# Rows of the split weights at four distances from the activations' edge

## The chip, the core and the metric

One Trainium2 chip, of which the kernel uses one core. A core has a matrix engine (TensorE, PE in the profile; its weight loads are listed apart as PEld), a vector engine (DVE), a scalar engine (ACT), a general engine (POOL) and a queue that starts transfers (SP). All of them read and write SBUF, the memory on the core, which has 128 partitions; PE writes its results to PSUM. The metric is the device time of one execution in microseconds (us); lower is better.

## The reference

Two blocks of a model are computed in float32 for 256 tokens of width 2048. The first block is attention with a window and a SwiGLU, the second a gated recurrence (mLSTM, computed here in one piece for the 256 tokens) and an attention over a band of chunks. Cut to its large products:

```
qkv = rms_norm(x, mixer_norm) @ w_qkv;   x = x + attention(qkv) @ w_o
h = rms_norm(x, ffn_norm)
x = x + (silu(h @ w_gate) * (h @ w_up)) @ w_down
proj = modulate(rmsnorm(x, g_pre[0])) @ a_w_in        # 2048 x 16400
x = x + gate0 * rmsnorm(mlstm(proj) @ a_w_out, g_post[0])
kv = modulate(rmsnorm(x, kv_g)) @ kv_w;   qz = modulate(rmsnorm(x, g_pre[1])) @ b_w_in
x = x + gate1 * rmsnorm(band_attention(qz, kv) @ b_w_out, g_post[1])
```

The shifts, scales and gates are products of one row (silu(c)) with 2048 x 6144 and 2048 x 4096 matrices, and are made on DVE, not on PE.

## The kernel before

**Split products.** Each float32 weight matrix is cut into pieces of 256 rows by 512 columns (a slot). A slot is loaded into a tile `w` of 128 partitions x 2 x 512 (4096 bytes in a partition). ACT writes its rounded half `wh` (type fp32r), DVE the rest `wl = w - wh`. The activations lie in four tiles of 128 x 16 x 256, split in the same way: `xh`, `xl` (a normalised input, transposed) and `ah`, `al` (the output of a mixer or of the SwiGLU). A product is then three matmuls: high by high, high by low, low by high.

**Two modes** (`products`, L267 to L281). In mode tok a row of `wh` or `wl` (512 columns, 2048 bytes in a partition) is streamed past 128 columns of the activations, which are the loaded weights of the matmul; the profile writes this `mm<-wh,xh` (streamed operand first, loaded one second), 128x512. A slot gives 12 such matmuls: 2 rows, 2 halves of the tokens, 3 products. In mode wst a row of the activations (256 columns, 1024 bytes) is streamed past 128 columns of `wh` or `wl`; the profile writes `mm<-xh,wh`, 128x256. A slot gives 24 such matmuls. Each matmul has one weight load of 128 x 128.

**Buffers.** `w` has 3 buffers, `wh` and `wl` 4 each (L151, L153), used in turn: slot j of the stream uses buffer j mod 4. The tiles `xh`, `xl`, `ah`, `al`, `big` (16384 bytes each in a partition), `w`, `wh`, `wl` and `mvt` (4096 bytes each) follow each other in SBUF, so every row of `wh` and `wl` begins a multiple of 512 bytes behind the first byte of `xh` (the activations' edge). The tiles behind them are smaller. Three kinds that take part in fp32r matmuls do not stand on such a multiple, in the program as built: `acch` and `accl` begin 192 bytes past a multiple of 256 behind that edge, `onesr` 128 bytes, and the `wgh`, `wgl` of `gates_task` 160 bytes.

**What sets the order.** The stream of slots is a list fixed in the program (`order`, `plan`); between two matmuls of the stream, `pump` puts in work of background tasks (attention, transposes, gates), by a simple clock kept while the program is written. Two such tasks return below. `mv_reduce` (L378) sums a partial result over partitions with two fp32r matmuls, `bg<-acch,onesr` and `bg<-accl,onesr`. `gates_task` does 48 fp32r matmuls of 256 columns with only 40 columns of loaded weights, `bg<-xh,wgh`.

**The end.** The last product (`b_w_out`, mode tok) is finished by `fin_half` (L1235): ACT squares a piece of the result and sums it (`sumsq`, L458; the squares themselves go to a tile `sq` that nobody reads), DVE multiplies by the gate.

All engine instructions stand on line 66 in the profile, the line of the helper that issues them; they are told apart by their tiles.

```
            wh = strm.tile([P, SL, CW], F32R, tag="wh", bufs=4, name="wh")
            S.copy(wh, w)
            wl = strm.tile([P, SL, CW], F32R, tag="wl", bufs=4, name="wl")
            V.tensor_sub(wl, w, wh.bitcast(F32))
```

Of the kernel before, what the change touches and what calls it, by code (L numbers as in the profile page):

```python
# [10 lines left out]
F32 = mybir.dt.float32  # L11
F32R = mybir.dt.float32r
# [6 lines left out]
P = 128  # L19
# [2 lines left out]
KD = D // P  # L22
SL = 2
CW = 512
NEG = -1.0e30
EPS = 1e-6
DFF = 5632
# [53 lines left out]
def kernel(ctx: ExitStack, tc: tile.TileContext, i: dict, out: bass.AP):  # L81
# [6 lines left out]
    strm = ctx.enter_context(tc.tile_pool(name="strm", bufs=1))  # L88
    rest = ctx.enter_context(tc.tile_pool(name="rest", bufs=1))
    small = ctx.enter_context(tc.tile_pool(name="small", bufs=4))  # L90
    psp = ctx.enter_context(tc.tile_pool(name="psp", bufs=8, space=PSUM))

    live = [0, 0]
    mmres = [4]
    ver = {"x": [0] * KD, "a": [0] * KD}
# [21 lines left out]
    xh = keep.tile([P, KD, T], F32R, name="xh")  # L117
# [20 lines left out]
    def stream_load(upto):  # L138
        while cnt["load"] < min(upto, len(order)):
            ch, s = order[cnt["load"]]  # L140
            w = strm.tile([P, SL, CW], F32, tag="w", bufs=3, name="w")
            ch.load(s, w)
# [3 lines left out]
    def stream_split(upto):  # L146
        while cnt["split"] < min(upto, len(order)):
            j = cnt["split"]
            w = loaded.pop(j)
            clk.cur = 0.0  # L150
            wh = strm.tile([P, SL, CW], F32R, tag="wh", bufs=4, name="wh")  # L151
            S.copy(wh, w)
            wl = strm.tile([P, SL, CW], F32R, tag="wl", bufs=4, name="wl")  # L153
            V.tensor_sub(wl, w, wh.bitcast(F32))
            split[j] = (wh, wl, clk.cur)
            cnt["split"] += 1
# [54 lines left out]
    def wload(w, r0, c0):  # L211
        def f(s, t):
            a = w[r0 + s * SL * P:r0 + (s + 1) * SL * P, c0:c0 + CW]
            nc.sync.dma_start(out=t, in_=a.rearrange("(k p) n -> p k n", p=P))
# [11 lines left out]
    def do_group(idxs):  # L226
        staged = len(idxs) > 1
        ch, s0 = order[idxs[0]]
        for k in range(s0 * SL, (s0 + len(idxs)) * SL):
            while ver[ch.need[0]][k] < ch.need[1][k]:  # L230
                stall()
        stream_load(idxs[0] + 1 + PF)
        stream_split(idxs[0] + 1 + SP)
        if s0 == 0:
            shp = [P, CW] if ch.mode == "tok" else [P, 2, T]
            while live[0] + live[1] > 6:
# [3 lines left out]
        for ts in ((0,), (1,)) if staged else ((0, 1),):  # L240
            for j, idx in enumerate(idxs):
                s = order[idx][1]
                if j and ts[0]:
                    stream_load(idx + 1 + PF)
                    stream_split(idx + SP)
                wh, wl, t_w = split.pop(idx) if ts[-1] else split[idx]
                for k in range(SL):
                    kt = s * SL + k
                    clk.cur = max(t_w, rdy[ch.need[0]][kt])
                    products(ch, kt, k, wh, wl, ts)  # L250
                    ch.k = kt + ts[-1]
                    if not staged:
                        mv_step()
                    if kt < ch.nk - 1:
                        pump()
            if s == ch.ns - 1:
                clk.cur = clk.eng["pe"]
                if ch.part is not None:
                    for t in ts:
                        ch.part(ch.ps, t)  # L260
                if ts[-1]:
                    if not (ch.done and ch.done(ch.ps)):
                        mm_free()
                    ch.ps = None
                pump()
# [52 lines left out]
    def mv_jobs():  # L318
        for lab, w, c0, b, kind, dst in (
                [("A", i["ada0"], j * CW, i["ada_b"][0:1, j * CW:(j + 1) * CW], "col", (0, j // 4, j % 4))  # L320
                 for j in range(8)]
# [134 lines left out]
        return b.rearrange("p a b -> p (a b)")  # L456

    def sumsq(junk_pool, src, dst, scale=1.0):  # L458
        j = junk_pool.tile([P, CW], F32, tag="sq", bufs=1, name="sq")
        S.activation(j, src, ACTF.Square, scale=scale, accum_out=dst)  # L460

    def xt_pair(m):
# [83 lines left out]
    ssx = rest.tile([P, 2, 4], F32, name="ssx")  # L546
# [208 lines left out]
    def resid(n, ps, pool, after):  # L755
        for t in range(2):
            c = x[:, t, n * CW:(n + 1) * CW]
            V.tensor_add(c, ps[t], c)
            sumsq(pool, c, ssx[:, t, n:n + 1])
        add_bg(after(n))  # L760
# [36 lines left out]
    pools = {}  # L797
# [50 lines left out]
    def down_part(ps, t):  # L848
        c = x[:, t, 3 * CW:]
        V.tensor_add(c, ps[t], c)  # L850
        sumsq(pools["q2"], c, ssx[:, t, 3:4])
        if t:
            add_bg(xt_raw(3, raw))
# [146 lines left out]
    def num_task(h, v):  # L1000
# [22 lines left out]
        for t in range(2):  # L1023
            sumsq(q3, nm[t], ss[:, t:t + 1], scale=rd[:, t:t + 1])
# [143 lines left out]
    def band_head(g, j):  # L1168
# [5 lines left out]
        nc.sync.dma_start(out=bi, in_=bass.AP(tensor=rel.tensor, offset=h * 383, ap=[[1, P], [1, T]]))  # L1174
        G.memset(bi[0:64, 0:64], NEG)
        yield 1
# [57 lines left out]

    def fin_half(ps, t, n):  # L1235
        c = pools["yy"][:, t, n * CW:(n + 1) * CW]
        sumsq(pools["q4"], ps[t], ssx[:, t, n:n + 1])
        V.tensor_mul(c, ps[t], gt[1][:, n * CW:(n + 1) * CW])

    def fin_done(n):  # L1240
        def f(ps):
            for t in range(2):
                fin_half(ps, t, n)
        return f

    def fin_part(ps, t):
        fin_half(ps, t, 3)
        x_rstd((t,))
        for n in range(4):
            c = x[:, t, n * CW:(n + 1) * CW]  # L1250
            y = pools["yy"][:, t, n * CW:(n + 1) * CW]
            if n == 3:
                S.activation(y, y, ACTF.Copy, scale=rst[:, t:t + 1])
                G.tensor_add(c, c, y)
            else:
                V.scalar_tensor_tensor(c, y, rst[:, t:t + 1], c, op0=ALU.mult, op1=ALU.add)
        for n in range(4):
            nc.sync.dma_start(out=out[t * P:(t + 1) * P, n * CW:(n + 1) * CW], in_=x[:, t, n * CW:(n + 1) * CW])
# [39 lines left out]
    S.activation(warm, ones[:, 0:1], ACTF.Exp)  # L1298
    stream_load(1)
    stream_split(1)  # L1300
    load_x(0)
    nc.sync.dma_start(out=cols, in_=i["cols"])
# [35 lines left out]
def _lay(inputs):  # L1338
# [10 lines left out]
    r = np.arange(P)  # L1349
    lo = np.where(r[None, :] <= r[:, None], f(0), f(NEG)).astype(f)  # L1350
    up = np.where(r[None, :] > r[:, None], f(0), f(NEG)).astype(f)
    ge = np.where(r[None, :] >= r[:, None], f(0), f(NEG)).astype(f)
    inv = np.power(10000.0, -np.arange(0, 64, 2) / 64.0).astype(f)
# [33 lines left out]
```

## Time and profile before

| | |
|---|---|
| time, median of 2 runs | 2506.33 us (2505.83 to 2506.83) |
| profiled execution, its own time | 2509.79 us |
| span of the profile | 2508.0 us |
| mean granted TensorE clock | 0.989 |
| PE busy, share of the span | 97% |
| DVE busy | 70% |
| ACT busy | 48% |
| transfers | 575.63 MB, 230 GB/s |

PE's matmuls overlap each other in the profile: the duration of a matmul (389 ns, say) is not what it costs in a dense stretch. That is the distance from its start to the start of the next one. The timeline prints starts to 0.01 us, so distances below are taken over several matmuls.

### The profile page before, as it was taken

What the parts mean: (1) busy time and instruction counts of PE and PEld (TensorE: products, weight loads), DVE (VectorE), ACT (ScalarE), POOL (GpSimd) and SP (SyncE); (2) the same over time, 40 slices, a digit from 0 to 9 for tenths busy, and PEclk for the clock granted to TensorE, in tenths of its full rate; (3) what the DMA queues carried; (4) which work ended last, traced back from release to release, by engine and by line L of the source; (5) the groups of instructions that cost most, each with busy time, mean ns of one, the idle gap of its engine ahead of it and who ended that gap; (6) DMA issues with size and microseconds to landing.
All of it is one profiled execution on the core that took longest, in us unless ns stands there. A gap on an engine that the chain in (4) does not pass through costs nothing.

```text
span 2508.0 us, 34570 instructions
## 1 busy us (share of the span) xinstructions
PE 2438.4 (97%) x12782; PEld 2076.4 (83%) x12782; DVE 1752.8 (70%) x2577; ACT 1210.1 (48%) x1654; POOL 173.4 (7%) x174
## 2 busy tenths in 40 slices
PE   8989999999999999899999999999999899999998
PEld 6867888887888888778888788888888789899986
DVE  6885777777777777768778777755454664577765
ACT  5665544334443444554445444445444544555553
POOL 0232000000000000201101100101101120000000
PEclk9989999999999999999999999999999999999999
DMA  6524788888888887568878788856556456678854
GB/s 211 157 96 143 238 285 284 286 275 279 287 283 291 285 286 267 159 213 269 264 250 273 267 286 277 261 170 192 182 169 196 151 151 186 193 254 263 259 188 153
DMA packets 319226, 575.63 MB, mean 230 GB/s; under 512 B 21680, under 2 KB 56752, under 8 KB 319056
## 3 DMA queue, kind: packets, MB, share of 16 engines
q1 hardware_dynamic: 319056, 573.42, 70.8%
q8 instruction: 100, 1.64, 0.3%
q14 instruction: 70, 0.57, 0.1%
HBM read 571.25 MB, written 2.10 MB: 229 GB/s over the span
## 4 chain that ended last, share of the span: by engine, by line
PE 77%; DVE 7%; DMA 6%; issue 4%; ACT 4%; POOL 2%; SPq 0%; ACTq 0%; DVEq 0%; POOLq 0%
PE mm L66 72%; PE bg L66 5%; DVE wl L66 3%; ACT wh L66 2%; DMA w<-in_a_w_in_dram 2%; DVE mvacc L66 2%; DMA w<-in_w_gate_dram 1%; DMA w<-in_w_down_dram 1%; POOL big L66 1%; DMA w<-in_w_qkv_dram 1%; ACT big L66 1%; POOL y L66 0%; DMA w<-in_a_w_out_dram 0%; POOL so L66 0%; ACT sq L66 0%
## 5 line engine op out<-in xcount | busy, mean ns | idle before, releaser
L66 DVE TENSOR_TENSOR wl<-w,wh 128x1024 fp32r<-128x1024 f32 x816 | 1009.3, 1244 | 620.9 <-ACT wh L66 605.4
L66 ACT CAST wh<-w 128x1024 fp32r<-128x1024 f32 x816 | 854.9, 1051 | 957.1 <-PE mm L66 598.8
L66 PE MATMUL mm<-wh,xh 128*128 128x512 f32 x1760 | 691.4, 393 | 0.0
L66 PE MATMUL mm<-wh,xl 128*128 128x512 f32 x1760 | 686.8, 390 | 3.8 <-DVE xl L66 3.8
L66 PE MATMUL mm<-wl,xh 128*128 128x512 f32 x1760 | 686.8, 390 | 3.0 <-DVE wl L66 3.0
L66 DVE SCALAR_TENSOR_TENSOR mvacc<-mvt,sc,mvacc 128x512 f32<-128x512 f32 x512 | 392.2, 766 | 10.1 <-issue 0.5
L66 PEld LDWEIGHTS mm<-wh,xl 128*128 128x128 f32 x1760 | 331.1, 188 | 74.3 <-DVE xl L66 4.7
L66 PEld LDWEIGHTS mm<-wl,xh 128*128 128x128 f32 x1760 | 331.2, 188 | 72.2 <-DVE wl L66 5.1
L66 PEld LDWEIGHTS mm<-wh,xh 128*128 128x128 f32 x1760 | 331.2, 188 | 70.5 <-issue 2.6
L66 PE MATMUL mm<-xh,wh 128*128 128x256 f32 x1280 | 370.0, 289 | 7.9 <-DVE xh L66 7.9
L66 PE MATMUL mm<-xl,wh 128*128 128x256 f32 x1280 | 367.5, 287 | 1.0 <-DVE xl L66 0.9
L66 PE MATMUL mm<-xh,wl 128*128 128x256 f32 x1280 | 365.6, 286 | 0.0
L66 PE MATMUL mm<-wh,al 128*128 128x512 f32 x864 | 337.8, 391 | 3.5 <-DVE al L66 3.5
L66 PE MATMUL mm<-wh,ah 128*128 128x512 f32 x864 | 340.3, 394 | 0.0
L66 PE MATMUL mm<-wl,ah 128*128 128x512 f32 x864 | 337.5, 391 | 0.0
L66 PEld LDWEIGHTS mm<-xh,wh 128*128 128x128 f32 x1280 | 249.2, 195 | 11.6 <-DVE xh L66 5.5
L66 PEld LDWEIGHTS mm<-xl,wh 128*128 128x128 f32 x1280 | 249.1, 195 | 4.4 <-DVE xl L66 3.5
L66 PEld LDWEIGHTS mm<-xh,wl 128*128 128x128 f32 x1280 | 249.1, 195 | 0.0
L66 PEld LDWEIGHTS mm<-wh,al 128*128 128x128 f32 x864 | 163.0, 189 | 38.1 <-DVE al L66 3.9
L66 PEld LDWEIGHTS mm<-wh,ah 128*128 128x128 f32 x864 | 162.9, 189 | 36.7 <-issue 3.3
L66 PEld LDWEIGHTS mm<-wl,ah 128*128 128x128 f32 x864 | 163.0, 189 | 33.2 <-DVE wl L66 0.3
L66 POOL TENSOR_TENSOR so<-so,sz 128x512 f32<-128x512 f32 x16 | 29.6, 1851 | 711.8 <-DVE mvacc L66 361.8
(191 smaller groups left out, 1303.2 us busy)
## 6 DMA issues: line engine op xcount, KB each, us to landing
mvt<-in_ada_dram SPq DMA_DIRECT2D x192, 512.0 KB
w<-in_a_w_in_dram SPq DMA_DIRECT2D x192, 512.0 KB
w<-in_w_gate_dram SPq DMA_DIRECT2D x88, 512.0 KB
w<-in_w_up_dram SPq DMA_DIRECT2D x88, 512.0 KB
w<-in_w_down_dram SPq DMA_DIRECT2D x88, 512.0 KB
mvt<-in_kv_ada_dram SPq DMA_DIRECT2D x64, 512.0 KB
w<-in_a_w_in_dram SPq DMA_DIRECT2D x128, 256.0 KB
w<-in_a_w_out_dram SPq DMA_DIRECT2D x64, 512.0 KB
```

The source lines that it names most:

```text
L66: return fn(*a, **k)
```

## The change

`wh` and `wl` get tiles that are 64 elements (256 bytes) longer, and the data begin 32, 8, 24 or 40 elements into them, by the number of the slot modulo 4. A tile of 4352 bytes is a multiple of 256, so the rows of the four buffers now begin 128, 32, 96 or 160 bytes past a multiple of 256 behind the activations' edge. The eight longer tiles take 2048 bytes more in a partition. These are won by having the squares of the last product written into `xh` in place of a tile `sq`. All that lies behind the eight tiles moves by 2048 bytes.

```
+ROOM = 64
+OFFS = (32, 8, 24, 40)
...
+    def offset_tile(tag, off):
+        t = strm.tile([P, SL * CW + ROOM], F32R, tag=tag, bufs=4, name=tag)
+        return t[:, off:off + SL * CW].rearrange("p (k n) -> p k n", n=CW)
...
-            wh = strm.tile([P, SL, CW], F32R, tag="wh", bufs=4, name="wh")
+            wh = offset_tile("wh", OFFS[j % 4])
             S.copy(wh, w)
-            wl = strm.tile([P, SL, CW], F32R, tag="wl", bufs=4, name="wl")
+            wl = offset_tile("wl", OFFS[j % 4])
             V.tensor_sub(wl, w, wh.bitcast(F32))
...
     def sumsq(junk_pool, src, dst, scale=1.0):
-        j = junk_pool.tile([P, CW], F32, tag="sq", bufs=1, name="sq")
+        if junk_pool is None:
+            j = xh[:, 0:2].rearrange("p k t -> p (k t)")
+        else:
+            j = junk_pool.tile([P, CW], F32, tag="sq", bufs=1, name="sq")
         S.activation(j, src, ACTF.Square, scale=scale, accum_out=dst)
...
-        sumsq(pools["q4"], ps[t], ssx[:, t, n:n + 1])
+        sumsq(None, ps[t], ssx[:, t, n:n + 1])
```

No instruction moves on any engine. The one place where the two programs' instructions read differently is on ACT, in the last product. Before, in ACT's order near its end (`sq` is the unread tile, `ssx` the sums, `mm` the result in PSUM):

```order
L66 CAST wh<-w 128x1024 x9
L66 ACTIVATE sq,ssx<-mm 128x512 x2
L66 CAST wh<-w 128x1024 x2
L66 ACTIVATE sq,ssx<-mm 128x512 x2
L66 CAST wh<-w 128x1024 x8
```

And at the same place of the changed program:

```order
L68 CAST wh<-w 128x1024 x9
L68 ACTIVATE xh,ssx<-mm 128x512 x2
L68 CAST wh<-w 128x1024 x2
L68 ACTIVATE xh,ssx<-mm 128x512 x2
L68 CAST wh<-w 128x1024 x8
```

The squares stand where they stood; only the tile that they write is another (and the helper's line is 68, since two lines were added above it).

## Rows read from the trace of the kernel before

**Rows 1.** The page's part 1: busy time, share of the span and instructions of three engines.

```profile
PE 2438.4 (97%) x12782; PEld 2076.4 (83%) x12782; DVE 1752.8 (70%) x2577; ACT 1210.1 (48%) x1654; POOL 173.4 (7%) x174
```

**Rows 2.** The windows view, five stretches: stretch, its length, busy time and count of PE, PEld, DVE, ACT and POOL, granted clock of TensorE, share of the DMA engines, GB/s. The stretches are first attention, SwiGLU, recurrence, band attention, and the last product.

```profile
core 0: us, PE busy (x) PEld busy (x) DVE busy (x) ACT busy (x) POOL busy (x), PEclk, DMA share, GB/s
0.00:290.00 290.00, 270.02 (x1285) 210.84 (x1286) 208.64 (x546) 172.72 (x352) 59.00 (x60) 0.97 0.50 159
290.00:1020.00 730.00, 723.60 (x3249) 598.81 (x3247) 549.16 (x625) 308.83 (x332) 7.91 (x15) 1.00 0.84 280
1020.00:2020.00 1000.00, 969.33 (x5013) 825.47 (x5014) 688.54 (x926) 487.06 (x627) 97.81 (x76) 0.98 0.70 223
2020.00:2410.00 390.00, 388.02 (x2850) 369.16 (x2849) 252.56 (x407) 200.73 (x288) 5.15 (x22) 1.00 0.70 221
2410.00:2508.00 98.00, 87.44 (x392) 72.16 (x390) 53.89 (x78) 40.72 (x56) 3.49 (x2) 0.97 0.50 164
```

**Rows 3.** The page's part 4, the chain of work that ended last, its shares by line; and one piece of the same chain in order of time: start us, length us, engine and group, count of instructions.

```profile
PE mm L66 72%; PE bg L66 5%; DVE wl L66 3%; ACT wh L66 2%; DMA w<-in_a_w_in_dram 2%; DVE mvacc L66 2%; DMA w<-in_w_gate_dram 1%; DMA w<-in_w_down_dram 1%; POOL big L66 1%; DMA w<-in_w_qkv_dram 1%; ACT big L66 1%; POOL y L66 0%; DMA w<-in_a_w_out_dram 0%; POOL so L66 0%; ACT sq L66 0%
```

```profile
730.55 130.61 PE mm L66 x576
```

**Rows 4.** The groups view, forms kept apart, the whole span: line, engine, operation, tiles, shape, count, busy us, mean ns of one, idle time before. Of each mode and activation the group high by high; the two other products of the same stream have the same count.

```profile
L66 PE MATMUL mm<-wh,xh 128*128 128x512 f32 x1760 | 691.4, 393 | 0.0
...
L66 PE MATMUL mm<-xh,wh 128*128 128x256 f32 x1280 | 370.0, 289 | 7.9 <-DVE xh L66 7.9
...
L66 PE MATMUL mm<-wh,ah 128*128 128x512 f32 x864 | 340.3, 394 | 0.0
```

**Rows 5.** The timeline of PE at a change from mode wst to mode tok: start us, duration us, engine, line, operation, tiles, shape, count. The first two rows are the first and the last of 31 matmuls in a row (30 steps), the other three the first, third and sixth of mode tok behind them.

```profile
2404.73 0.28 PE L66 MATMUL mm<-xh,wl 128*128 128x256 f32 x1
...
2408.33 0.28 PE L66 MATMUL mm<-xh,wl 128*128 128x256 f32 x1
2408.45 0.40 PE L66 MATMUL mm<-wh,ah 128*128 128x512 f32 x1
...
2408.92 0.39 PE L66 MATMUL mm<-wh,al 128*128 128x512 f32 x1
...
2409.61 0.39 PE L66 MATMUL mm<-wh,al 128*128 128x512 f32 x1
```

**Rows 6.** The timeline of PE where the pair acch, accl stands in a stream of mode tok (columns as in group 5). From the first row to the last there are 12 steps: one matmul of the stream, the pair, 9 matmuls of the stream.

```profile
1487.00 0.40 PE L66 MATMUL mm<-wh,al 128*128 128x512 f32 x1
1487.23 0.28 PE L66 MATMUL bg<-acch,onesr 128*128 128x256 f32 x1
1487.35 0.28 PE L66 MATMUL bg<-accl,onesr 128*128 128x256 f32 x1
1487.46 0.40 PE L66 MATMUL mm<-wh,ah 128*128 128x512 f32 x1
...
1489.54 0.39 PE L66 MATMUL mm<-wh,ah 128*128 128x512 f32 x1
```

**Rows 7.** The same pair in a stream of mode wst: 12 steps from the first row to the last (the pair, then 10 matmuls of the stream), 9 of them from the second row to the third.

```profile
1531.86 0.28 PE L66 MATMUL bg<-acch,onesr 128*128 128x256 f32 x1
...
1532.09 0.28 PE L66 MATMUL mm<-xh,wh 128*128 128x256 f32 x1
...
1533.15 0.28 PE L66 MATMUL mm<-xh,wh 128*128 128x256 f32 x1
1533.28 0.28 PE L66 MATMUL mm<-xl,wh 128*128 128x256 f32 x1
```

**Rows 8.** The timeline of PE in `gates_task`: the first and the last of 48 matmuls in a row (47 steps).

```profile
1060.97 0.28 PE L66 MATMUL bg<-xh,wgh 128*40 128x256 f32 x1
...
1066.46 0.28 PE L66 MATMUL bg<-xh,wgl 128*40 128x256 f32 x1
```

**Rows 9.** The windows view for three short stretches (columns as in group 2), and the timeline of PE in the first of them: the first and the last of 10 matmuls in a row (9 steps).

```profile
1247.00:1249.00 2.00, 2.00 (x11) 2.00 (x11) 2.00 (x4) 0.61 (x1) 0.00 (x0) 0.50 0.83 256
1138.00:1144.00 6.00, 6.00 (x52) 6.00 (x52) 5.63 (x4) 4.73 (x7) 3.64 (x3) 1.00 0.83 269
...
740.00:860.00 120.00, 120.00 (x531) 99.38 (x530) 91.03 (x100) 47.84 (x47) 1.58 (x3) 1.00 0.87 289
```

```profile
1247.13 0.41 PE L66 MATMUL mm<-xl,wh 128*128 128x256 f32 x1
...
1249.06 0.41 PE L66 MATMUL mm<-xl,wh 128*128 128x256 f32 x1
```

**Rows 10.** The groups view, the whole span (columns as in group 4): the two splits of the weights, and a rounding beside a plain copy of one shape on ACT.

```profile
L66 DVE TENSOR_TENSOR wl<-w,wh 128x1024 fp32r<-128x1024 f32 x816 | 1009.3, 1244 | 620.9 <-ACT wh L66 605.4 <-PE mm L66 10.6 <-PE bg L66 0.5
L66 ACT CAST wh<-w 128x1024 fp32r<-128x1024 f32 x816 | 854.9, 1051 | 957.1 <-PE mm L66 598.8 <-DMA w<-in_a_w_in_dram 112.0 <-DMA w<-in_w_up_dram 43.6
...
L66 ACT CAST ah<-bg 128x512 fp32r<-128x512 f32 x46 | 25.1, 589 | 39.3 <-PE bg L66 39.1
...
L66 ACT COPY big<-bg 128x512 f32<-128x512 f32 x32 | 17.2, 593 | 12.3 <-PE bg L66 12.1
```

**Rows 11.** The view of one tile: the squares of the last product (tile sq), and the last matmuls that read the tile xh: engine, operation, tiles, count, durations ns min/median/max, first and last start us, forms.

```profile
L66 ACT ACTIVATE sq<-mm x8: 597/598/599, 2447.8 to 2497.8; 128x512 f32<-128x512 f32 x8
```

```profile
L66 PE MATMUL mm<-xh,wl x24: 278/283/283, 2399.8 to 2408.3; 128*128 128x256 f32 x24
```

## Prediction

> **What bounds the kernel now.** I read the page's busy times first: PE is busy for 97% of the span, DVE for 70%, ACT for 48% [rows 1]. The stretches show that this holds in each stage: in the SwiGLU PE is busy for 723.6 of 730 us at the full clock, while the DMA engines are at 0.84 [rows 2]. The chain that ended last is 72% matmuls of the stream (`PE mm`); no wait in it has more than 3% [rows 3]. So the question is what one matmul of the stream costs, from its start to the next start.
>
> There are 3 x (1760 + 864) = 7872 matmuls of mode tok and 3 x 1280 = 3840 of mode wst [rows 4]. In mode tok a piece of the chain has 576 of them in 130.61 us, that is 0.2267 us each [rows 3]. In mode wst 30 steps take 3.60 us, 0.1200 us each [rows 5]. Together 7872 x 0.2267 + 3840 x 0.1200 = 1785 + 461 = 2246 us, nine tenths of the span. Of these, 72% of 2508 us, or 1806 us, lie on the chain: 0.80. I count a gain or loss on a matmul at 0.80.
>
> At the full clock of 2.4 GHz 512 columns stream in 213.3 ns and 256 in 106.7 ns. So a matmul pays 13.4 ns beyond its columns in one mode and 13.3 ns in the other: the same price for twice the columns, one per matmul and weight load. It isn't a fixed number of array cycles: where the granted clock is 0.50 (1.2 GHz, after PE had stood still), 9 steps of mode wst take 1.93 us, 0.2144 us each, against 213.3 ns for the columns alone [rows 9]. There the price is gone, within the 1 ns that the printed starts allow. Something outside the array, that matters only when it takes operands at full speed, sets it. The change touches only where operands lie, and this is the one price that it could touch.
>
> **The change part by part.** *Order.* No instruction or wait moves; buffers are as many as before.
>
> *The splits.* ACT and DVE write the same shapes at other places. No row here shows a write at a shifted place; I take 1051 and 1244 ns as they are [rows 10]. If they grew, cover is there: ACT idled 957 us ahead of these rows, 599 of them because the buffer was still in use by PE, and DVE 621 us for ACT. In the other direction, writes do not disturb PE: from 1138 to 1144 us DVE, ACT and POOL are busy for 5.63, 4.73 and 3.64 of 6 us, and PE has 52 matmuls in the window at an even step [rows 9]. Price 0.
>
> *The squares in `xh`.* Eight of them, 598 ns each, the first at 2447.8 us; the last matmul that reads `xh` starts at 2408.3 us [rows 11], so their wait for it ended 39 us earlier. Writing to an fp32r tile costs ACT no more than to a float32 tile, 589 against 593 ns for one shape [rows 10]. Price 0. Without that cover the first square would hold ACT's queue and the two last splits behind it; nothing here comes near.
>
> *The distance.* What a shifted operand costs is not shown for this stream. The nearest rows are pairs that the stream itself contains. `acch`, `accl` and their loaded `onesr` lie 192 and 128 bytes past a multiple of 256, everything around them lies on one. In mode tok the 12 steps around such a pair take 2.54 us [rows 6]; 10 even steps of 0.2267 and 2 of 0.1200 would be 2.507. So it costs 0.033 us, and the pair itself does not: its steps are 0.12 and 0.11. The loss comes behind it: the 9 next matmuls, whose own operands lie as ever, take 2.08 us, 0.2311 each, and then the even step is back. In mode wst 12 steps take 1.42 us against 1.44 even, a gain of 0.02, and the 9 steps behind the pair run at 1.06/9 = 0.1178 us [rows 7]. The even step is a rhythm that is lost by another distance and found again within ten matmuls; without it mode tok is slower by 4.4 ns, mode wst faster by 2.2 ns. A change of mode does the same: wst to tok costs 1.16 - 5 x 0.2267 = 0.027 us in five steps [rows 5].
>
> The new kernel changes the distance at each new slot: 7872/12 = 656 times in mode tok, 3840/24 = 160 times in mode wst. Lower bound: the distance does nothing, 0. Upper bound of this kind: each change of slot costs what the pair costs, 656 x 0.033 = +21.6 us, and 160 x -0.02 = -3.2 us. That the rhythm never returns gives nearly the same: 7872 x 4.4 ns = +34.6 and 3840 x -2.2 ns = -8.4, so +26 us before the factor. I take half of the pair's price, since nothing tells which of the four steps (128, 32, 96, 160) disturb: +10.8 - 1.6 = +9.2 us, times 0.80 = +7.4 us.
>
> The sum: the profiled execution's own time is 2509.8 us, 3.5 above the median of the runs. 2509.8 + 7.4 = 2517.2 us, or 2514 us at the level of the median.
>
> **A rule against any effect.** The trace shows a price of 13.3 ns per matmul with its weight load and rhythms that change when loaded and streamed operands lie otherwise [rows 5 to 7]. The Trainium skill, "TensorE: Matmul & The Clock Gate", Part 2, says that the engine reads the streamed and the loaded operand through two independent ports, so that loading the next weights takes nothing from the running matmul. "SBUF — State Buffer", Specifications (TRN2), gives lines of 16 bytes as the only unit in a row, and all four distances are multiples of it. By both the sum would be 0 and the time 2506 us; the first of them does not fit the pair of rows 6. That case is the first rival.
>
> **The rivals.** *Nothing happens:* the rhythm depends only on when operands are read, and a stream that keeps one distance for 12 or 24 matmuls stays in it. 2506 us. For it: with 52 matmuls in 6 us nothing else in SBUF disturbs PE [rows 9]. Against it: rows 6 and 7.
>
> *Faster:* the 13.3 ns come from loaded and streamed rows meeting in SBUF when they lie on the same edge, and another distance sheds them. For it: the price goes with the load, not the columns, and vanishes at the half clock; and steps with operands elsewhere cost less, 5.49/47 = 0.1168 us with 40 loaded columns, where an even step is 0.1200 [rows 8], and 0.11 us behind `accl` [rows 6]. Against it: the pair itself gains only a few ns, and mode tok then loses. Prices: 3.2 ns on all 11712 matmuls x 0.80 = -30 us; the whole 13.3 ns, -125 us, 2381 us; two distances in four shedding it, -62 us, 2444 us. It passes 2% at 50/(0.80 x 11712) = 5.3 ns per matmul. The DMA engines would have room: 0.87 from 740 to 860 us [rows 9].
>
> *Slower:* each distance settles mode tok in a worse rhythm than the uneven mean. The worst steps in the rows are the two from 2408.45 to 2408.92 us, 0.235 each, 8.3 ns over the even step [rows 5]. On all 7872: +65 x 0.80 = +52 us, 2558 us. It decides from 50/(0.80 x 7872) = 7.9 ns. For it: mode tok is two thirds of the matmuls and has so far only lost by a disturbance. Against it: such steps came two in a row, never as a lasting one.
>
> **How the numbers follow.** A 2% change is 50 us, about what a measurement of this kernel can tell from no change. A small loss, 2500 to 2535 us: 0.43. Nothing happens: 0.15. Faster: 0.31, of which 0.28 by over 2%. Slower rhythm: 0.11, of which about 0.10 over 2%. Within 2%, then: 0.43 + 0.15 + 0.03 + 0.01 = 0.62. The range from 2415 to 2548 us takes in half of the faster case's span and the never-even bound with something over; it leaves out about 0.1 on each side.
>
> **What would show it.** Right: steps of mode tok between 0.227 and 0.231 us, uneven behind a change of slot and even again before the next; mode wst at 0.118 to 0.120; ACT's and DVE's splits at 1051 and 1244 ns. The faster rival shows as a mode tok step under 0.221 in the slots of one or more distances, with other slots unchanged; the slower one as a lasting 0.234. Wrong altogether would be a longer `wh` or `wl` row, a stage that starts to wait for DMA, or squares that wait for PE.

## The result and the profile after

The changed kernel takes 2537.85 us (median of 2 runs, 2537.37 to 2538.32) against 2506.33 us: a ratio of 1.0126 with a 95% interval of 1.0101 to 1.015. It is 31.5 us slower, which lies within 2% and well outside the scatter of the runs. The profiled execution has its own time of 2537.37 us, a span of 2535.6 us and a mean granted clock of 0.991; before, the span was 2508.0 us.

Part 1 of the page (busy time, share of the span, instructions), to be set beside [rows 1]:

```profile
PE 2472.9 (98%) x12782; PEld 2068.0 (82%) x12782; DVE 1756.4 (69%) x2577; ACT 1206.7 (48%) x1654; POOL 172.8 (7%) x174
```

PE is busy for 34.5 us more, with the same 12782 instructions; DVE and ACT each differ by under 4 us. The time in which PE has nothing in it fell from 2508.0 - 2438.4 = 69.6 us to 62.7 us. So PE's own instructions became slower, and some 7 us of that were taken out of waits that PE had before. The stretches show where (windows view, columns as in [rows 2]; the first two stretches are the same as there, the others are set later by what the stages were late):

```profile
0.00:290.00 290.00, 269.69 (x1278) 207.17 (x1279) 208.37 (x545) 171.19 (x352) 58.06 (x60) 0.98 0.51 158
290.00:1020.00 730.00, 729.75 (x3190) 589.31 (x3189) 542.44 (x598) 300.92 (x321) 7.88 (x15) 1.00 0.84 277
1020.00:2030.00 1010.00, 984.81 (x5020) 822.76 (x5018) 684.94 (x924) 483.95 (x623) 86.17 (x63) 0.99 0.70 222
```

In the second stretch, the SwiGLU, PE left 6.4 of 730 us empty before and leaves 0.25 now, and yet gets through 3190 matmuls in place of 3249. The clock is 1.00 in both. Not all of the 6.15 us between them is gained: waits of 0.68 and 2.34 us near the end of the stretch are there in both kernels, but 16 us later in the changed one, which puts them behind 1020 us. Waits of 2.91 and 0.33 us for the tile `sg` are really gone. The larger of each pair, in the timeline of PE (the last bracket is PE's idle time before the row, and what ended it), first in the kernel before:

```profile
595.35 0.33 PE L66 MATMUL bg<-kc,sg 128*128 128x128 f32 x1 [2.91 <-DVE sg L66]
...
1020.70 1.19 PE L66 MATMUL bg<-dg,onesr 128*128 128x256 f32 x2 [2.34 <-DVE dg L66]
```

And in the changed kernel:

```profile
602.12 1.03 PE L68 MATMUL bg<-kc,sg 128*128 128x128 f32 x8
...
1036.89 1.22 PE L68 MATMUL bg<-dg,onesr 128*128 128x256 f32 x2 [2.34 <-DVE dg L68]
```

Two pieces of the chain of work that ended last (start us, length us, engine and group, count) give the step of each mode. The first is the dense piece of mode tok that [rows 3] show for before, the second a piece of 96 matmuls of mode wst:

```profile
740.21 134.23 PE mm L68 x576
...
2397.13 11.41 PE mm L68 x96
```

And the same piece of mode wst in the kernel before:

```profile
2371.59 11.51 PE mm L66 x96
```

Mode tok went from 130.61/576 = 0.2267 to 134.23/576 = 0.2330 us a matmul, mode wst from 11.51/96 = 0.1199 to 11.41/96 = 0.1189. Whether mode tok finds the even step again within a slot is read from PE's timeline (columns as in [rows 5]), where each row shown stands 12 steps, one slot's worth, behind the one before it:

```profile
740.28 0.39 PE L68 MATMUL mm<-wl,ah 128*128 128x512 f32 x1
...
743.07 0.39 PE L68 MATMUL mm<-wl,ah 128*128 128x512 f32 x1
...
745.86 0.40 PE L68 MATMUL mm<-wl,ah 128*128 128x512 f32 x1
...
748.66 0.39 PE L68 MATMUL mm<-wl,ah 128*128 128x512 f32 x1
...
751.45 0.40 PE L68 MATMUL mm<-wl,ah 128*128 128x512 f32 x1
```

The four stretches take 2.79, 2.79, 2.80 and 2.79 us, where 12 even steps are 2.72. Each of the four distances loses 0.07 to 0.08 us in a slot, twice what the pair of [rows 6] cost in all. The splits did not change (part 5 of the page of after, columns as in [rows 10]), nor did the squares, which now go to `xh` (the view of the tile xh, columns as in [rows 11]):

```profile
L68 DVE TENSOR_TENSOR wl<-w,wh 128x1024 fp32r<-128x1024 f32 x816 | 1009.5, 1244 | 642.7 <-ACT wh L68 632.4
L68 ACT CAST wh<-w 128x1024 fp32r<-128x1024 f32 x816 | 852.1, 1048 | 985.7 <-PE mm L68 728.6
```

```profile
L68 ACT ACTIVATE xh<-mm x8: 597/599/601, 2474.1 to 2525.4; 128x512 fp32r<-128x512 f32 x8
```

The splits last 1048 and 1244 ns as before; what grew is ACT's idle time until PE gives a buffer back, 728.6 us against 598.8. That is what a slower PE looks like from the engine that feeds it.

### The profile page after: what moved, and what is told of

It reads as the page before. It is cut to its first block, busy times and chain, and to the rows that moved or that the text cites. A ratio compares the mean times of both kernels' runs of the same rounds, so it can differ in the third digit from the quotient of the medians.

```text
span 2535.6 us, 34570 instructions
## 1 busy us (share of the span) xinstructions
PE 2472.9 (98%) x12782; PEld 2068.0 (82%) x12782; DVE 1756.4 (69%) x2577; ACT 1206.7 (48%) x1654; POOL 172.8 (7%) x174
## 4 chain that ended last, share of the span: by engine, by line
PE 81%; DVE 5%; DMA 4%; issue 4%; ACT 3%; POOL 1%; SPq 0%; ACTq 0%; DVEq 0%; POOLq 0%
PE mm L68 76%; PE bg L68 5%; DMA w<-in_a_w_in_dram 3%; DVE wl L68 2%; ACT wh L68 2%; DVE mvacc L68 1%; DMA w<-in_w_qkv_dram 1%; POOL big L68 0%; POOL so L68 0%; ACT big L68 0%; POOL y L68 0%; DMA w<-in_a_w_out_dram 0%; DVE xl L68 0%; ACT sq L68 0%; DMA mvacc<-in_ada_b_dram 0%
## 5 line engine op out<-in xcount | busy, mean ns | idle before, releaser
L68 DVE TENSOR_TENSOR wl<-w,wh 128x1024 fp32r<-128x1024 f32 x816 | 1009.5, 1244 | 642.7 <-ACT wh L68 632.4
L68 ACT CAST wh<-w 128x1024 fp32r<-128x1024 f32 x816 | 852.1, 1048 | 985.7 <-PE mm L68 728.6
L68 PE MATMUL mm<-wh,xh 128*128 128x512 f32 x1760 | 701.4, 399 | 0.0
L68 PE MATMUL mm<-wh,xl 128*128 128x512 f32 x1760 | 695.8, 395 | 4.3 <-DVE xl L68 4.3
L68 PE MATMUL mm<-wl,xh 128*128 128x512 f32 x1760 | 695.9, 395 | 1.8 <-DVE wl L68 1.7
```

Of the source, the lines that this page charges most:

```text
L68: return fn(*a, **k)
```

## The experiments

Four theories stood to be told apart. The **change theory** is the one of the prediction: the even step is a rhythm that each new distance disturbs. The **distance theory**: a distance that is not a multiple of 256 bytes spoils the step, whether or not it changes. The **pair theory** and the **place theory** say what kind of distance that is: between the streamed and the loaded row of a matmul, or of a row from a fixed edge of SBUF. All runs below keep the stream, the waits and the arithmetic; offsets are in elements of 4 bytes.

| run | time, us | before on the same chip, us | ratio (95% interval) | dense piece of mode tok |
|---|---|---|---|---|
| c0 | 2505.74 | 2504.48 | 1.0007 (0.9994 to 1.0021) | 130.59/576 = 0.2267 |
| c128 | 2535.23 | 2504.48 | 1.0129 (1.0094 to 1.0164) | 133.85/576 = 0.2324 |
| c32 | 2540.84 | 2504.48 | 1.0152 (1.012 to 1.0183) | 134.39/576 = 0.2333 |
| scan16 | 2527.47 | 2504.48 | one run | by distance, below |
| shift128 | 2506.58 | 2505.93 | 1.0 (0.9988 to 1.0011) | 130.59/576 = 0.2267 |
| wl128 | 2540.73 | 2505.93 | 1.0139 (1.0119 to 1.0159) | 134.40/576 = 0.2333 |
| mode64 | 2496.81 | 2505.93 | 0.9956 (0.994 to 0.9972) | 130.59/576 = 0.2267 |
| scan4 | 2539.18 | 2505.93 | one run | by distance, below |
| mode76 | 2494.27 | 2508.16 | 0.9934 (0.9911 to 0.9956) | 130.59/576 = 0.2267 |
| scanrest | 2544.8 | 2508.16 | one run | by distance, below |

**c0: all that the change does, but no distance.** Longer tiles and squares in `xh`, offsets of zero. (The tiles of 4352 bytes now put the four buffers alternately 0 and 256 bytes past a multiple of 512.)

```
-OFFS = (32, 8, 24, 40)
+OFFS = (0, 0, 0, 0)
```

> All four slots at distance 0, with the longer tiles and the squares in xh kept: the change without its distances. Both theories (the change theory: a new distance at each slot keeps the even rhythm from coming back; the distance theory: a row that lies off the edge has a worse step of its own, kept or changed) expect 2504 to 2509 us, mode tok at 0.2267 us a step and mode wst at 0.1200. If the squares or the moved tiles cost something, it is above 2512.

The chain of c0:

```profile
725.89 130.59 PE mm L68 x576
...
2369.60 11.51 PE mm L68 x96
```

The time is that of before, and so is the step of both modes. The longer tiles, the moved tiles behind them and the squares cost nothing, and 256 bytes of distance are as good as 512.

**c128 and c32: one distance that never changes.**

```
-OFFS = (32, 8, 24, 40)
+OFFS = (32, 32, 32, 32)
```

> All four slots at 128 bytes, one distance for the whole stream. Change theory: the rhythm is found once and kept, 2503 to 2512 us, mode tok at 0.2267, mode wst at 0.1200. Distance theory: as in the changed kernel in the slots of this distance, mode tok at about 0.232 and mode wst at about 0.1186, 2530 to 2540 us.

```
-OFFS = (32, 8, 24, 40)
+OFFS = (8, 8, 8, 8)
```

> All four slots at 32 bytes. Change theory: 2503 to 2512 us with even steps of 0.2267 and 0.1200. Distance theory: uneven steps, mode tok at about 0.233 and mode wst at about 0.118, 2532 to 2545 us. If this one is uneven and the kernel with 128 bytes even, it is the place within 64 bytes that counts.

Both are as slow as the change, with no change of distance between slots. Two pieces of the chain of c128, some 270 us apart:

```profile
467.64 133.86 PE mm L68 x576
...
739.06 133.85 PE mm L68 x576
```

The even piece has 130.59. In 576 matmuls that all lie at one distance the rhythm is not found again. The change theory falls; the distance theory stands.

In c128 `wh` and `wl` also lie 128 bytes further from `w`, which ACT and DVE read while they write the two halves, so the splits might disturb PE in a way that they don't in c0. The trace speaks against it. Worked out from the timeline of c128, 266 steps of mode tok pass while ACT, DVE and POOL all stand still; they average 232.3 ns, where all dense steps of that mode average 232.5. In the kernel before, 184 such steps average 226.9 and all of them 227.0.

**shift128: everything moves together.** The kernel before, with 128 bytes of unused tile ahead of `xh`: all of the activations, `w`, `wh` and `wl` lie 128 bytes further on, and their distances to each other are as before.

```
+    pad = keep.tile([P, 32], F32, name="pad")
```

> The kernel before with a tile of 128 bytes ahead of the activations, so that activations and split weights all move by 128 bytes and the distance between them stays a multiple of 512. Two theories are left. Pair theory: what counts is the distance between the streamed row and the row that is loaded meanwhile; even steps of 0.2267 and 0.1200, 2500 to 2510 us. Place theory: what counts is where in 256 bytes a streamed row begins; mode tok at about 0.2325, mode wst (its streamed rows move too) no longer at 0.1200, 2530 us or more.

```profile
726.14 130.59 PE mm L66 x576
...
2375.57 11.51 PE mm L66 x96
```

The even steps of both modes (the chain of shift128) and the time are those of before. The place theory falls, as far as this one shift can tell: what counts is how the streamed and the loaded rows lie to each other, the pair theory. Whether it is the row that the matmul itself has loaded, or the one that is being loaded for the next matmul meanwhile, no run separates.

**wl128: only `wl` at a distance.** `wh` at 0, `wl` at 128 bytes, so one product in three has a distance and two have none.

```
+            wh = offset_tile("wh", 0)
...
+            wl = offset_tile("wl", 32)
```

> Only wl at 128 bytes, wh at 0: one matmul in three has a pair off the edge. If a step depends on its own pair alone, the steps that stream wl in mode tok are at about 0.2325 and the others at 0.2267, mean 0.2286: 2513 to 2520 us. If a step off the rhythm upsets the next ones too, as behind the pair acch, accl, all three kinds are uneven, mean 0.231 or more: 2525 to 2540 us.

The chain of wl128:

```profile
740.41 134.40 PE mm L67 x576
...
2397.91 11.44 PE mm L67 x96
```

The loss is not a third of that of c128; it is all of it (0.2333 against 0.2324 in this piece, 232.7 against 232.5 ns over all dense steps of mode tok). The time, 2540.73 us, is just over the range that was expected for this case. Worked out from the timeline, start to start in dense stretches, the steps from high-by-high to `wl`, from `wl` to high-by-low, and from there to the next high-by-high average 234.5, 233.0 and 230.7 ns in mode tok; all three are over the even 226.7. A matmul whose own operands lie well is slow behind one whose operands do not. The price is not one of a matmul by itself. This agrees with the pair `acch`, `accl` of [rows 6], where the loss lay in the nine matmuls behind it.

**scan16, scan4, scanrest: many distances in one kernel.** Each distance is kept for a block of slots; scan16 goes through the 16 multiples of 16 bytes, the two others through multiples of 4 bytes, counted apart for each mode.

```
+OFFS = tuple(4 * n for n in range(16))
...
+            wh = offset_tile("wh", OFFS[j // 17 % 16])
```

> Sixteen distances, 0 to 240 bytes in steps of 16, each kept for 17 slots in a row. Change theory: every block runs even after its first ten matmuls, 2505 to 2515 us. Distance theory: the blocks at 0 bytes run at 0.2267 and 0.1200, the others each at a step of their own, mode tok mostly at 0.231 to 0.235; 2525 to 2545 us. A block below 0.2267 in mode tok or below 0.117 in mode wst would show a distance that is better than none.

```
+OFF_TOK = (57, 58, 59, 60, 61, 62, 63, 64, 1, 2, 3, 14, 15, 16, 17, 18)
+OFF_WST = (12, 13, 14, 15, 16, 17, 18, 19, 20, 52, 53, 54, 55, 56, 57, 58)
...
+            off = OFF_WST[n // 10] if mode == "wst" else OFF_TOK[n // 41]
```

> Finer scan: in mode tok 41 slots at each of 228 to 256 bytes, then 4, 8, 12, then 56 to 72, in steps of 4; in mode wst 10 slots at each of 48 to 80, then 208 to 232. Pair theory: 256 bytes as 0 (0.2267 even); near it a range of even steps, since 240 was even; near 64 in mode wst a minimum at or under 0.115. Change and place theories have no forecast beyond 0.231 to 0.235 in mode tok off the edge. Time 2500 to 2520 us.

> The 35 multiples of 4 bytes not yet tried in mode tok, 19 slots at each, and 32 of those in mode wst, 5 slots at each. Pair theory has no forecast for one of them; from the distances so far, mode tok 0.228 to 0.238, mode wst 0.113 to 0.121, time 2525 to 2550 us. A distance under 0.2267 in mode tok would point to a faster kernel; if none is, distance 0 is the best place for that mode.

Mean steps in ns by distance in bytes, worked out from the timeline (start to start of two matmuls of the stream that follow each other in one mode, those left out that take over 45 ns more than their columns; one kernel each, so a distance with two rhythms can differ between runs):

| mode, run | distance: step |
|---|---|
| tok, scan16 | 0: 227.3, 16: 231.7, 32: 233.2, 64: 229.4, 96: 233.4, 128: 232.3, 160: 234.2, 208: 234.7, 240: 227.5 |
| tok, scan4 | 4: 237.2, 60: 227.3, 64: 229.4, 68: 235.9, 240: 236.6, 244: 239.8, 252: 227.8 |
| tok, scanrest | 20: 238.7, 28: 227.3, 76: 228.4, 100: 239.8, 108: 227.4, 156: 227.9, 196: 239.7 |
| wst, scan16 | 0: 120.0, 32: 118.4, 64: 114.9, 96: 118.6, 128: 118.6, 160: 120.0, 208: 116.9 |
| wst, scan4 | 52: 114.0, 64: 113.5, 72: 118.5, 76: 113.4, 216: 119.8, 220: 120.6 |
| wst, scanrest | 24: 121.2, 88: 113.9, 140: 120.0, 148: 116.8 |

No distance makes mode tok faster than 0 does; many make it slower, by up to 13 ns. Mode wst has distances that save 6 ns. The table shows a choice of the distances. All of them, sorted by what is left of the distance when it is divided by 16 bytes (mean steps in ns, worked out in the same way; a distance tried twice counts with its mean; the lowest and the highest are of single blocks):

| remainder, bytes | tok: mean (lowest to highest), distances | wst: mean, distances |
|---|---|---|
| 0 | 232.2 (227.3 to 236.6), 16 | 118.3, 16 |
| 4 | 237.0 (233.4 to 239.8), 16 | 118.3, 15 |
| 8 | 233.2 (231.0 to 235.5), 16 | 118.3, 15 |
| 12 | 229.3 (227.3 to 232.4), 16 | 118.4, 13 |

So mode tok has an order: every distance with remainder 12 is faster than every one with remainder 4, and that is why neighbours 4 bytes apart (96 and 100, say) can differ by more than distances far apart. Mode wst has no such order; its fast distances (52, 64, 76, 88) have four different remainders. All four distances of the change have remainder 0.

Forecasts for the scans failed in places. scan4 took 2539.18 us, 19 us more than the top of its range, and the range of even steps that it expected around 256 bytes is not there (244 has 239.8 ns, 240 has 236.6). In scanrest the steps of mode tok go from 227.3 to 239.8 ns, somewhat beyond 228 to 238. The next rows (PE's timeline, columns as in [rows 5]) are the first and the last matmul of blocks at one distance. In scanrest 125 steps of mode tok at 100 bytes:

```profile
696.71 0.40 PE L69 MATMUL mm<-wl,xh 128*128 128x512 f32 x1
...
726.70 0.40 PE L69 MATMUL mm<-wh,xh 128*128 128x512 f32 x1
```

That is 29.99/125 = 0.2399 us each, a lasting slow step. At 240 bytes the same distance gives two different steps. In scan16, 204 steps of mode tok:

```profile
799.20 0.40 PE L68 MATMUL mm<-wh,ah 128*128 128x512 f32 x1
...
845.45 0.40 PE L68 MATMUL mm<-wh,xh 128*128 128x512 f32 x1
```

And in scan4, 317 steps:

```profile
469.44 0.40 PE L69 MATMUL mm<-wl,ah 128*128 128x512 f32 x1
...
544.46 0.40 PE L69 MATMUL mm<-wh,ah 128*128 128x512 f32 x1
```

46.25/204 = 0.2267 in the one, 75.02/317 = 0.2367 in the other. So a distance has more than one rhythm that it can stay in, and what went before seems to decide which; that last point was not tested by itself.

**mode64 and mode76: what the scans point to.** Mode tok at 0, mode wst at 64 or at 76 bytes.

```
+            off = 19 if order[j][0].mode == "wst" else 0
+            wh = offset_tile("wh", off)
...
+            wl = offset_tile("wl", off)
```

(In mode64 the 19 is 16.)

> Slots of mode tok at distance 0, slots of mode wst at 64 bytes, by the scan's steps. Pair theory: mode tok at 0.2267, mode wst at 0.115 instead of 0.1200, so 3840 x 5.1 ns x 0.80 = 16 us less than before, ratio 0.992 to 0.996. Place theory expects the same here, since only the loaded rows of mode wst move; it would not if the streamed operand alone counted (ratio 1.000).

> As the kernel with 64 bytes in mode wst, with 76 bytes there instead. In the finer scan the blocks at 76 bytes ran even at 0.1134, those at 64 fell in two states, 0.1135 there and 0.1158 in the kernel with 64 alone. Pair theory, if the even step holds through the stage: 3840 x 6.6 ns x 0.80 = 20 us less than before, ratio 0.990 to 0.994, mode wst at 0.1134. If the state depends on what went before, mode wst at 0.115 to 0.118 and a ratio of 0.995 to 0.997.

Both beat the kernel before, mode76 by 13.9 us (ratio 0.9934, 0.9911 to 0.9956) where 20 were forecast, mode64 by 9.1 where 16 were forecast. The timeline of PE shows the first and the last of one stretch of 598 matmuls of mode wst (597 steps), in mode64:

```profile
2032.55 0.29 PE L67 MATMUL mm<-xh,wl 128*128 128x256 f32 x1
...
2102.86 0.28 PE L67 MATMUL mm<-xh,wl 128*128 128x256 f32 x1
```

And in mode76:

```profile
2034.20 0.28 PE L67 MATMUL mm<-xh,wl 128*128 128x256 f32 x1
...
2101.86 0.28 PE L67 MATMUL mm<-xh,wl 128*128 128x256 f32 x1
```

70.31/597 = 0.1178 us a step against 67.66/597 = 0.1133. At 64 bytes this stretch is in an uneven rhythm, though others in the same run have 0.1133 and the mean over all is 115.9 ns; at 76 bytes the mean over all is 113.8. The step of 0.1133 is 6.7 ns over the 106.7 ns of 256 columns, where the kernel before pays 13.3: half of the price that the prediction set out from can be shed in this mode. Worth 3840 x 6.6 ns = 25 us at most, it gave 13.9. Part 1 of the page of mode76:

```profile
PE 2421.0 (97%) x12782; PEld 2057.8 (82%) x12782; DVE 1753.3 (70%) x2577; ACT 1209.3 (48%) x1654; POOL 173.8 (7%) x174
```

PE's busy time fell by 17.4 us (2438.4 to 2421.0), the span of the profile by 11.5 (2508.0 to 2496.5); the rest became waits of PE.

## Why the prediction was right or wrong

**The direction and the range were right, the range in part by luck.** A small loss was forecast as likeliest and came; within 2%, and 2537.85 lies between 2415 and 2548 us. The time was 24 us off the predicted 2514, and the loss was four times the predicted one (31.5 against 7.4 us). It lies above every case of the prediction's likeliest mechanism, whose own range ended at 2535 us; only the room left above the never-even bound takes it in.

**What bounds the kernel: right.** The time goes by PE's step. The 34.5 us that PE is busy longer carry the whole of the loss.

**Edits at price 0: right.** Splits 1048 and 1244 ns, squares 599 ns; c0 has them all without the distance and takes as long as before.

**The failed step is "I take half of the pair's price".** The prediction had the rhythm "lost by another distance and found again within ten matmuls", and so counted 656 changes of slot. c128 and c32 show that it is not the change that costs: at a distance of 128 or 32 bytes kept throughout, the even step never comes back. The nine steps behind the pair [rows 6] were read as the time in which a rhythm heals; by c128 and c32 they could heal since the operands lay at 0 again, and in the new stream they don't. The prediction had priced this very case, "that the rhythm never returns", as a bound, at +26 us before the factor of 0.80, or +21.

**That bound too was small.** It took 4.4 ns a matmul from the nine steps; measured are 0.2330 - 0.2267 = 6.3 ns in mode tok. For mode wst it took -2.2 ns; measured are -1.0 (0.1189 against 0.1199). The sum with the measured steps is 7872 x 6.3 - 3840 x 1.0 = 49.6 - 3.8 = +45.8 us, times 0.80 = +37 us, where 31.5 were measured. The factor would have to be 0.69. Part of that is seen: PE's empty time fell by 6.9 us, since a slower PE spends time in which it had waited before. The waits for `sg` in the SwiGLU are 3.2 us of that; where the rest of the difference went was not traced.

**Nothing happens: wrong.** c128 differs from c0 in the distance alone, and its interval of 1.0094 to 1.0164 lies apart from c0's of 0.9994 to 1.0021. The Trainium skill, "TensorE: Matmul & The Clock Gate", Part 2, has the streamed and the loaded operand read through two independent ports. These runs do not agree that the one therefore leaves the other alone, since 128 bytes of distance between them make a step 5.7 ns longer (133.85 against 130.59 us for 576), while 128 bytes for both together change nothing. The Trainium skill, "SBUF — State Buffer", Specifications (TRN2), has lines of 16 bytes. The prediction's step from there, that four multiples of 16 would change nothing, is wrong by the same runs. In mode tok the remainder by 16 bytes does sort the steps (237.0 ns at 4, 229.3 at 12), in mode wst it does not; no run shows whether these lines are the reason.

**Faster: wrong for this change, right for another.** The sign that the prediction gave, a step of mode tok under 0.221, is found at no distance of the three scans; the lowest is the even 0.2267. But that rival's mechanism, that another distance sheds part of the 13.3 ns, holds for mode wst at 52, 64, 76 and 88 bytes. None of the change's four distances is among these.

**Slower rhythm: its mechanism exists, not at these distances.** Lasting steps of 0.2367 and 0.2399 stand in the rows of scan4 and scanrest. The change's own four distances lie at 0.2330 on the average, 6.3 ns over the even step, below the 7.9 ns from which that rival passes 2%.

**The sign given for "right" was half met.** Mode wst at 0.118 to 0.120 and the splits were as written; mode tok is outside 0.227 to 0.231 and is not even again before the next slot.

**What stays open.** Why an even step exists at some distances and not at others, why mode tok goes by the remainder of 16 bytes and mode wst does not, and what picks one of two rhythms at one distance. The runs tell that the distance between streamed and loaded rows decides, and that a matmul at a bad distance slows those behind it. They do not show what inside the chip does it.

## What to carry to other kernels

Where PE runs matmuls with a weight load for each, back to back, the distance in SBUF between the streamed and the loaded rows is worth trying: here it moved a step by -6 to +13 ns at one instruction count. Mode tok went by the remainder of the distance by 16 bytes, mode wst by no order that was found, so scan it with blocks of slots in one kernel and read start-to-start distances by block. Keep two modes apart, since the best distance of one is not that of the other (0 is the best of mode tok and among the slowest of mode wst), and look for one that gives the same step in every block. A disturbance that dies away in a trace shows what the stream returns to, not that it would return to it if the disturbance stayed.

## What was not expected of the hardware

- At the full clock the operands' distance counts down to 4 bytes, the finest step that was tried: 96 and 100 bytes give 233.4 and 239.8 ns in mode tok, 104 and 108 give 231.0 and 227.4. In that mode the remainder by 16 bytes sorts them, with means of 232.2, 237.0, 233.2 and 229.3 ns for 0, 4, 8 and 12.
- A distance can carry more than one lasting step: 0.2267 and 0.2367 at 240 bytes in mode tok, 0.1133 and 0.1178 at 64 bytes in mode wst.
- One product in three at a bad distance costs as much as all three (wl128 and c128).
- The price of 13.3 ns beyond the columns is not a floor: mode wst runs 597 steps at 0.1133 us, 6.7 ns over its columns.
